# Entry of an MLP: the order of the last norms, where sums of weights are made, and where later columns of weights are put

## The chip, the cores and the metric

The kernel runs on one core of a Trainium2 chip. The metric is the device time of one execution in microseconds, the median of several runs. Before the change it is 1577.01 us (three runs, 1576.17 to 1580.71). The profile is of one further execution of the same program, 1580.5 us, whose span from the first instruction to the last is 1578.7 us.

## The reference

One transformer block in fp32 on 1024 tokens of width 1024: a projection, sparse and sliding-window attention, two gates, an output projection, and an MLP. What matters here is the end:

```python
h = h + rms_norm(y @ w_out[l], norm_mix_post[l])
u = rms_norm(h, norm_mlp_pre[l])
f = jnp.square(jax.nn.relu(u @ w_mlp_in[l])) @ w_mlp_out[l]
h = h + rms_norm(f, norm_mlp_post[l])
```

`w_mlp_in` is 1024 x 4096, `w_mlp_out` 4096 x 1024.

## The kernel before

Every fp32 product is made of three matmuls in the fp32r type: each operand is split into a high part (a copy to fp32r by ScalarE, line L87) and a low part (operand less high part, by VectorE or GpSimd, L91), and high x high, high x low and low x high are added in PSUM. `split` does both. In the names of the rows a final h or l stands for these parts: `ws_h` and `ws_l`, `bh` and `bl`.

The product `u @ w_mlp_in` is done by a scheme with seven products of blocks in place of eight. The right factor is u, transposed, cut into four blocks: upper and lower half of the 1024 rows of the contraction, and first and second 512 tokens. The weights are taken 256 columns at a time; such a *pair* p (16 in all) has two tiles of 128 columns, `raw[0]` and `raw[1]`, each with an upper half (a11, a21) and a lower one (a12, a22). Right factors 1 and 2 are blocks of the first tokens as they are; factors 5, 3, 6, 4 and 7 are made of sums and differences of the blocks. Left factors for 5, 6, 3 and 7 are sums and differences of the weights, four instructions per pair: `ws = a21 + a22` (L1012) and three subtractions (L1039), all on GpSimd. Each product has 12 matmuls of 128 x 128 by 128 x 512. `c11`, `c12`, `c21` and `c22` are the four results of a pair; relu and square follow, and further sums of them (`q`) go to memory as left factors of the second matrix product, which begins when all pairs are done.

In time the part that is changed runs like this. `out_proj` makes the product with `w_out` for blocks of 128 tokens, two at a time. A block b goes through `norm_a` (L854: residual; L856: squares), `norm_b` (L862: the normalised block, tile `o1`, `o` in the rows) and `norm_t` (TensorE's eight transposes L872 into `pt`; for b of 4 to 7 then `t1`, the difference to the block of the first tokens, L881, and copies into `b12` and `b22`, `b_h` and `b_l` in the rows; `t1` is split into factor 5). `factor(i, b)` makes one block of right factor i: 3 is only a split, 6 has two subtractions and a split (L893, L894), 4 one subtraction and a split (L897) and a copy (L899), 7 a split. A product with factor i needs all four blocks of it.

The products 1 and 2 of the first four pairs need the first tokens alone. They are made ahead by `head`, while blocks 4 to 7 are still in the norms: head p splits the first weight tile of pair p, runs the 24 matmuls, adds to get `c11` (L973), takes relu and square in one VectorE instruction (L974), and stores `c11` from SP's queue (L975). Then `mlp1` does the rest of each pair. Pairs 0 and 1 take turns, product by product, with the factors between them; the later pairs follow one by one. `mlp1` loads both tiles of its pair from SP's queue (L1008) into two places each for `wraw` and `wraw2`, so pair 2 loads into what pair 0 used.

The order on each engine is not that of the code. When the program is built, a scheduler places the instructions by their dependencies and by when it thinks that they can run; each engine then works strictly in its own order. SP's queue too: a transfer that waits for its place holds up those behind it. `tc.issue_after(x)` adds one rule: what is written under it stands behind x on x's engine. Tiles of one tag share its `bufs` places in turn: the heads' split weights have two places each for `wh` and `wl`.

Of the kernel before, what the change touches and what calls it, by code (L numbers as in the profile page):

```python
# [52 lines left out]
def tile_hybrid_block(ctx: ExitStack, tc: tile.TileContext, x, norm_mix_pre, norm_mix_post, norm_mlp_pre,  # L53
# [686 lines left out]
    with ExitStack() as s:  # L740
# [99 lines left out]

        ss2s = {}

        def load_x(b, eng=None):
# [15 lines left out]
        def norm_b(b):  # L859

            r2 = rstd_of(ep, ss2s[b])
            nc.vector.scalar_tensor_tensor(o1[b], hbs[b], r2, gpre, op0=ALU.mult, op1=ALU.mult)  # L862

        def norm_t(b):

            t = o1[b]
            bs = slice((b % 4) * P, (b % 4 + 1) * P)
            pts = []
            for k0 in range(0, NB, 4):
                pt = pp.tile([P, 4, P], F32, name="pt", tag="pt", bufs=2)  # L870
                for j in range(4):
                    nc.tensor.transpose(pt[:, j, :], t[:, (k0 + j) * P:(k0 + j + 1) * P], ident)  # L872
                if b < 4:
                    split(bh0[:, k0:k0 + 4, bs], bl0[:, k0:k0 + 4, bs], pt)
                    nc.scalar.activation(braw[b, k0 // 4], pt, AF.Copy)
                pts.append(pt)
            if b < 4:
                return

            t1 = eh.tile([P, 4, P], F32, name="t1", tag="hb", bufs=2)  # L880
            nc.vector.tensor_tensor(t1, pts[0], braw[b % 4, 0], op=ALU.subtract)  # L881
            nc.scalar.activation(b12[:, :, bs], pts[0], AF.Copy)
            nc.scalar.activation(b22[:, :, bs], pts[1], AF.Copy)
            split(bh[5][:, :, bs], bl[5][:, :, bs], t1)
# [59 lines left out]
        norm_a(6)  # L944
        norm_a(7)
        norm_t(4)

# [15 lines left out]
        def head(p, fp_, whl):  # L963
# [9 lines left out]
            nc.vector.tensor_tensor(c11, yb, s1, op=ALU.add)  # L973
            nc.vector.scalar_tensor_tensor(c11, c11, 0.0, c11, op0=ALU.max, op1=ALU.mult)  # L974
            nc.sync.dma_start(f_d[0][p], c11)  # L975
            pre[p] = xb, c11, s1
# [3 lines left out]
        for p in range(NPRE):  # L980
            head(p, fp0, load_wcols(w_mlp_in, 2 * p * P, P, wp2, rpool=wp2, l_eng="dve"))
            if p == 0:
                norm_t(5)
                norm_b(6)
                norm_b(7)
            if p == 1:
                norm_t(6)
                norm_t(7)
        for b in range(4):
            factor(3, b)  # L990
        s_e.close()
# [9 lines left out]

        def mlp1(p):
            raw = []
            for e in range(2):
                r = wp2.tile([P, NB, P], F32, name="wraw", tag="wraw", bufs=2) if e == 0 else \
                    w1a.tile([P, NB, P], F32, name="wraw2", tag="wraw2", bufs=2)
                c0 = (2 * p + e) * P
                nc.sync.dma_start(r, w_mlp_in[:, c0:c0 + P].rearrange("(k p) c -> p k c", p=P))  # L1008
                raw.append(r)
            a11, a12, a21, a22 = raw[0][:, 0:4], raw[0][:, 4:8], raw[1][:, 0:4], raw[1][:, 4:8]  # L1010
            sm = w1a.tile([P, 4, P], F32, name="ws", tag="ws", bufs=3)
            nc.gpsimd.tensor_tensor(sm, a21, a22, op=ALU.add)  # L1012
            early = p in pre
# [24 lines left out]
            for o, i0, i1 in ((sm, sm, a11), (a12, a12, sm), (a21, a11, a21)):  # L1038
                nc.gpsimd.tensor_tensor(o, i0, i1, op=ALU.subtract)  # L1039
            yb = ps_any()  # L1040
# [32 lines left out]
        for i in (6, 4, 7, 0, 0):  # L1073
            for g in two:
                next(g)
            for b in range(4 if i else 0):
                factor(i, b)
        for p in range(2, NPAIR):
# [193 lines left out]
```

## Time and profile before

| | |
|---|---|
| median of 3 runs | 1577.01 us |
| profiled execution | 1580.5 us, span 1578.7 us |
| TensorE busy | 1487.3 us, 94% |
| VectorE busy | 1088.4 us, 69% |
| ScalarE busy | 751.2 us, 48% |
| GpSimd busy | 439.8 us, 28% |
| first head's first matmul | 912.68 us |
| second matrix product of the MLP begins | 1262.36 us |

Busy shares are averages over the whole span. For one stage one asks for the stretch alone: how much of it each engine was busy, which clock TensorE was granted (1.00 is 2.4 GHz, 0.50 is 1.2 GHz), and what ended each idle time. A row in order of time has start, duration, engine, line, operation, out<-in and shapes; in square brackets stands the idle time of the engine before it and what it waited for. The rows of a stretch overlap by some hundredths, since an instruction begins while the one before it still drains; the distance of starts is what an instruction costs.

### The profile page before, as it was taken

What the parts mean: (1) busy time and instruction counts of PE and PEld (TensorE: products, weight loads), DVE (VectorE), ACT (ScalarE), POOL (GpSimd) and SP (SyncE); (2) the same over time, 40 slices, a digit from 0 to 9 for tenths busy, and PEclk for the clock granted to TensorE, in tenths of its full rate; (3) what the DMA queues carried; (4) which work ended last, traced back from release to release, by engine and by line L of the source; (5) the groups of instructions that cost most, each with busy time, mean ns of one, the idle gap of its engine ahead of it and who ended that gap; (6) DMA issues with size and microseconds to landing.
All of it is one profiled execution on the core that took longest, in us unless ns stands there. A gap on an engine that the chain in (4) does not pass through costs nothing. (4 is left out here: it accounts for less than half of the span.)

```text
span 1578.7 us, 20103 instructions
## 1 busy us (share of the span) xinstructions
PE 1487.3 (94%) x6920; PEld 1214.2 (77%) x6920; DVE 1088.4 (69%) x2086; ACT 751.2 (48%) x1461; POOL 439.8 (28%) x354
## 2 busy tenths in 40 slices
PE   6998999999899999999988978999999899999997
PEld 5897888878777777778866766778888688888886
DVE  5455775598964998836537787877757566594775
ACT  5343675576653766653336563332222334334543
POOL 3000351132310232231133014867555410000302
PEclk9999999999999999999999998999999999999999
DMA  7733125111132111164256652444443598263451
GB/s 201 256 103 82 38 51 154 41 44 31 34 97 51 47 34 31 34 225 139 94 186 229 225 159 58 158 162 156 147 153 134 208 336 302 94 188 118 150 184 54
DMA packets 162038, 204.79 MB, mean 130 GB/s; under 512 B 15120, under 2 KB 105264, under 8 KB 161936
## 3 DMA queue, kind: packets, MB, share of 16 engines
q1 hardware_dynamic: 154224, 180.68, 36.5%
q0 software_dynamic: 6992, 20.48, 3.7%
q10 hardware_dynamic: 720, 2.36, 0.4%
q8 instruction: 54, 0.88, 0.2%
q14 instruction: 48, 0.39, 0.1%
HBM read 153.02 MB, written 58.32 MB: 134 GB/s over the span
## 5 line engine op out<-in xcount | busy, mean ns | idle before, releaser
L124 PE MATMUL mm<-uh,wh 128*128 128x512 f32 x464 | 201.4, 434 | 4.1 <-DVE qb L448 3.2
L510 POOL TENSOR_TENSOR e<-e,w 128x256 f32<-128x256 f32 (+7 forms) x128 | 111.6, 898 | 286.4 <-DVE w L648 148.9
L125 PE MATMUL mm<-ul,wh 128*128 128x512 f32 x464 | 184.9, 398 | 0.0
L126 PE MATMUL mm<-uh,wl 128*128 128x512 f32 x464 | 184.5, 398 | 0.0
L87 ACT ACTIVATE th<-pt 128x512 fp32r<-128x512 f32 (+1 forms) x178 | 105.1, 593 | 95.0 <-PE pt L520 84.9
L502 ACT ACTIVATE e<-e,nm 128x256 f32<-128x256 f32 (+7 forms) x192 | 124.4, 649 | 36.8 <-DVE nm L496 36.4
L91 DVE TENSOR_TENSOR tl<-pt,th 128x512 fp32r<-128x512 f32 x162 | 110.0, 682 | 33.8 <-ACT th L87 32.7
L87 ACT ACTIVATE fh<-fraw 128x1024 fp32r<-128x1024 f32 x56 | 59.4, 1062 | 145.3 <-PE xs L1165 78.3
L87 ACT ACTIVATE wh<-wraw 128x1024 fp32r<-128x1024 f32 x69 | 73.0, 1058 | 111.1 <-PE mm L125 36.7
L91 DVE TENSOR_TENSOR fl<-fraw,fh 128x1024 fp32r<-128x1024 f32 x56 | 69.2, 1241 | 78.2 <-ACT fh L87 78.2
L520 PE MATMUL pt<-ident,e 128*128 128x128 f32 x648 | 104.8, 276 | 1.9 <-DVE e L513 0.9
L1165 PE MATMUL xs<-vl,fh 128*128 128x512 f32 x256 | 100.7, 393 | 4.2 <-DVE vl L91 4.2
L126 PEld LDWEIGHTS mm<-uh,wl 128*128 128x128 f32 x464 | 88.0, 190 | 20.9
L124 PEld LDWEIGHTS mm<-uh,wh 128*128 128x128 f32 x464 | 88.9, 192 | 17.4 <-issue 3.3
L91 DVE TENSOR_TENSOR wl<-wraw,wh 128x1024 fp32r<-128x1024 f32 x53 | 69.0, 1301 | 45.9 <-ACT wh L87 45.5
L1165 PE MATMUL xs<-vh,fl 128*128 128x512 f32 x256 | 100.5, 393 | 0.0
L1165 PE MATMUL xs<-vh,fh 128*128 128x512 f32 x256 | 100.2, 392 | 0.0
L1188 POOL TENSOR_TENSOR cc<-cc,gB 128x512 f32<-128x512 f32 x14 | 24.3, 1759 | 269.0 <-ACT sq L1187 267.3
L520 PEld LDWEIGHTS pt<-ident,e 128*128 128x128 f32 x648 | 81.7, 141 | 22.7 <-issue 2.5
L125 PEld LDWEIGHTS mm<-ul,wh 128*128 128x128 f32 x464 | 89.0, 192 | 12.0
L116 POOL TENSOR_TENSOR wl<-wraw,wh 128x384 fp32r<-128x384 f32 (+2 forms) x26 | 38.7, 1493 | 161.7 <-ACT wh L108 161.7
L91 POOL TENSOR_TENSOR wl<-wraw,wh 128x1024 fp32r<-128x1024 f32 x16 | 38.6, 2410 | 159.5 <-ACT wh L87 159.5
(286 smaller groups left out, 4086.0 us busy)
## 6 DMA issues: line engine op xcount, KB each, us to landing
fraw<-f_d SPq DMA_DIRECT2D x48, 512.0 KB, 3.6
wraw<-in_w_mlp_in_dram SPq DMA_DIRECT2D x36, 512.0 KB, 4.5
wraw<-in_w_out_dram SPq DMA_DIRECT2D x32, 512.0 KB, 3.6
f_d<-q SPq DMA_DIRECT2D x64, 256.0 KB, 3.6
b<-in_w_mlp_out_dram SPq DMA_DIRECT2D x32, 512.0 KB, 10.8
wraw<-in_w_in_dram SPq DMA_DIRECT2D x27, 512.0 KB, 4.7
f_d<-c SPq DMA_DIRECT2D x48, 256.0 KB, 4.0
gate_d<-gst SPq DMA_DIRECT2D x32, 256.0 KB, 2.1
```

Source lines behind the costliest of these rows:

```text
L87: nc.scalar.activation(h, src, AF.Copy)
L91: eng.tensor_tensor(l, src, h.bitcast(F32), op=ALU.subtract)
L116: eng.tensor_tensor(lv[:, a:b], rv[:, a:b], hv[:, a:b].bitcast(F32), op=ALU.subtract)
L124: nc.tensor.matmul(ps, ah, bh, start=first, stop=False)
L125: nc.tensor.matmul(ps, ah, bl, start=False, stop=False)
L126: nc.tensor.matmul(ps, al, bh, start=False, stop=last)
L502: nc.scalar.activation(e[:, :n], e[:, :n], AF.Exp, scale=-1.0, bias=nm[:, r:r + 1], accum_out=sm[:, r:r + 1])
L510: nc.gpsimd.tensor_tensor(res[r][:, :n], res[r][:, :n], w[:, r:r + 1].to_broadcast([P, n]), op=ALU.mult)
L520: tr = nc.tensor.transpose(pt[:rows, r, :], es[r][:, off:off + rows], ident)
L1165: nc.tensor.matmul(bank[t], l_[:, j, ts], r_[:, j, :], start=a_, stop=z_, skip_group_check=True)
L1188: (nc.vector if b == NB - 1 else nc.gpsimd).tensor_tensor(cc[:, ns], cc[:, ns], gB[:, ns], op=ALU.mult)
```

## The change

It has four parts.

- `norm_b` of blocks 6 and 7 moves in the code from behind head 0 to the place behind their `norm_a`, and the factors are told to stand behind them on VectorE: factor 3 behind the last `norm_b`, factors 6, 4 and 7 behind the last `t1`.
- For the four early heads, relu and square of `c11` become two instructions on ScalarE, and `c11` is stored from GpSimd's queue.
- The tiles of weights of pairs 0 to 3 are loaded by `load_raw` ahead of all `mlp1`, in the order of the pairs as far as their places allow. Pairs 2 and 3 get places of their own: those of the heads' split weights (`wraw3`, in the tags `wh` and `wl`).
- For pairs 0 and 1 the sum `ws` and the three subtractions run on VectorE, for the others on GpSimd as before.

```diff
@@ -839,6 +839,7 @@
                     nc.vector.tensor_tensor(o1[b][:, ns], pss[t, nh], gpost[:, ns], op=ALU.mult)
 
         ss2s = {}
+        last_norm, last_t = [None], [None]
 
         def load_x(b, eng=None):
             hbs[b] = hb_e[b] if b in hb_e else (eh if b < 4 else ea).tile([P, D], F32, name="hb", tag="hb", bufs=2)
@@ -859,7 +860,7 @@
         def norm_b(b):
 
             r2 = rstd_of(ep, ss2s[b])
-            nc.vector.scalar_tensor_tensor(o1[b], hbs[b], r2, gpre, op0=ALU.mult, op1=ALU.mult)
+            last_norm[0] = nc.vector.scalar_tensor_tensor(o1[b], hbs[b], r2, gpre, op0=ALU.mult, op1=ALU.mult)
 
         def norm_t(b):
 
@@ -878,7 +879,7 @@
                 return
 
             t1 = eh.tile([P, 4, P], F32, name="t1", tag="hb", bufs=2)
-            nc.vector.tensor_tensor(t1, pts[0], braw[b % 4, 0], op=ALU.subtract)
+            last_t[0] = nc.vector.tensor_tensor(t1, pts[0], braw[b % 4, 0], op=ALU.subtract)
             nc.scalar.activation(b12[:, :, bs], pts[0], AF.Copy)
             nc.scalar.activation(b22[:, :, bs], pts[1], AF.Copy)
             split(bh[5][:, :, bs], bl[5][:, :, bs], t1)
@@ -943,6 +944,8 @@
         load_x(7)
         norm_a(6)
         norm_a(7)
+        norm_b(6)
+        norm_b(7)
         norm_t(4)
 
 
@@ -971,8 +974,12 @@
             prod(yb, wh[:, 4:8, :], wl[:, 4:8, :], 2, True, True)
             c11 = fp_.tile([P, 512], F32, name="c11", tag="c11", bufs=NPRE + 1)
             nc.vector.tensor_tensor(c11, yb, s1, op=ALU.add)
-            nc.vector.scalar_tensor_tensor(c11, c11, 0.0, c11, op0=ALU.max, op1=ALU.mult)
-            nc.sync.dma_start(f_d[0][p], c11)
+            if p < NPRE:
+                nc.scalar.activation(c11, c11, AF.Relu)
+                nc.scalar.activation(c11, c11, AF.Square)
+            else:
+                nc.vector.scalar_tensor_tensor(c11, c11, 0.0, c11, op0=ALU.max, op1=ALU.mult)
+            (nc.gpsimd if p < NPRE else nc.sync).dma_start(f_d[0][p], c11)
             pre[p] = xb, c11, s1
 
         s_f0 = s.enter_context(ExitStack())
@@ -981,13 +988,12 @@
             head(p, fp0, load_wcols(w_mlp_in, 2 * p * P, P, wp2, rpool=wp2, l_eng="dve"))
             if p == 0:
                 norm_t(5)
-                norm_b(6)
-                norm_b(7)
             if p == 1:
                 norm_t(6)
                 norm_t(7)
-        for b in range(4):
-            factor(3, b)
+        with tc.issue_after(last_norm[0].ins):
+            for b in range(4):
+                factor(3, b)
         s_e.close()
 
         s_m1 = s.enter_context(ExitStack())
@@ -999,17 +1005,28 @@
             return (p_.tile([P, 4, P], F32R, name=tag + "h", tag=tag + "h", bufs=bufs),
                     p_.tile([P, 4, P], F32R, name=tag + "l", tag=tag + "l", bufs=bufs))
 
-        def mlp1(p):
+        def load_raw(p):
+
             raw = []
             for e in range(2):
-                r = wp2.tile([P, NB, P], F32, name="wraw", tag="wraw", bufs=2) if e == 0 else \
-                    w1a.tile([P, NB, P], F32, name="wraw2", tag="wraw2", bufs=2)
+                if p in (2, 3):
+                    r = wp2.tile([P, NB, P], F32, name="wraw3", tag="wl" if e else "wh", bufs=2)
+                else:
+                    r = (w1a if e else wp2).tile([P, NB, P], F32, name="wraw2" if e else "wraw",
+                                                 tag="wraw2" if e else "wraw", bufs=2)
                 c0 = (2 * p + e) * P
                 nc.sync.dma_start(r, w_mlp_in[:, c0:c0 + P].rearrange("(k p) c -> p k c", p=P))
                 raw.append(r)
+            return raw
+
+        raws = {p: load_raw(p) for p in range(NPRE)}
+
+        def mlp1(p):
+            raw = raws[p] if p in raws else load_raw(p)
             a11, a12, a21, a22 = raw[0][:, 0:4], raw[0][:, 4:8], raw[1][:, 0:4], raw[1][:, 4:8]
             sm = w1a.tile([P, 4, P], F32, name="ws", tag="ws", bufs=3)
-            nc.gpsimd.tensor_tensor(sm, a21, a22, op=ALU.add)
+            diff = nc.vector if p < 2 else nc.gpsimd
+            diff.tensor_tensor(sm, a21, a22, op=ALU.add)
             early = p in pre
             if early:
                 xb, c11, _ = pre[p]
@@ -1036,7 +1053,7 @@
             yield
 
             for o, i0, i1 in ((sm, sm, a11), (a12, a12, sm), (a21, a11, a21)):
-                nc.gpsimd.tensor_tensor(o, i0, i1, op=ALU.subtract)
+                diff.tensor_tensor(o, i0, i1, op=ALU.subtract)
             yb = ps_any()
             prod(yb, *left(3, a12), 3, True, True)
             c12 = ft("c")
@@ -1073,8 +1090,9 @@
         for i in (6, 4, 7, 0, 0):
             for g in two:
                 next(g)
-            for b in range(4 if i else 0):
-                factor(i, b)
+            with tc.issue_after(last_t[0].ins):
+                for b in range(4 if i else 0):
+                    factor(i, b)
         for p in range(2, NPAIR):
             for _ in mlp1(p):
                 pass
```

On VectorE, in the norms of blocks 6 and 7 (`hb_8978` and `o1_8894` belong to block 6, `hb_8980` and `o1_8901` to block 7; `braw` holds the blocks of the first tokens), the kernel before has, from the residual of block 7 on:

```order
L854 SCALAR_TENSOR_TENSOR hb_8980<-o1_8901,rs_o_9008,hb_8980 128x1024
L153 RECIPROCAL rs_o_9095<-rs_a_9093 128x1
L91 TENSOR_TENSOR wl_9220<-wraw_9217,wh_9219 128x1024
L974 SCALAR_TENSOR_TENSOR c11_9143<-c11_9143 128x512
L91 TENSOR_TENSOR bl6_8919<-braw_8028,bh6_8918 128x4x128
L91 TENSOR_TENSOR bl4_8921<-braw_8029,bh4_8920 128x4x128
L894 TENSOR_TENSOR braw_8030<-b_l_8923,braw_8030 128x512
L862 SCALAR_TENSOR_TENSOR o1_8894<-hb_8978,rs_o_9095,gpre_8043 128x1024
L973 TENSOR_TENSOR c11_9213<-ps_9200,s1_9198 128x512
L147 TENSOR_SCALAR rs_t_9100<-ss2_9011 128x1
L149 RECIPROCAL rs_r_9102<-rs_s_9098 128x1
L897 TENSOR_TENSOR braw_8031<-braw_8030,braw_8031 128x512
```

The kernel after has there:

```order
L976 TENSOR_TENSOR c11_9144<-ps_9131,s1_9129 128x512
L863 SCALAR_TENSOR_TENSOR o1_8894<-hb_8978,rs_o_9022,gpre_8043 128x1024
L147 TENSOR_SCALAR rs_t_9027<-ss2_9011 128x1
L91 TENSOR_TENSOR wl_9223<-wraw_9220,wh_9222 128x1024
L149 RECIPROCAL rs_r_9029<-rs_s_9025 128x1
L151 SCALAR_TENSOR_TENSOR rs_a_9031<-rs_r_9029,rs_t_9027,rs_s_9025 128x1
L153 RECIPROCAL rs_o_9033<-rs_a_9031 128x1
L863 SCALAR_TENSOR_TENSOR o1_8901<-hb_8980,rs_o_9033,gpre_8043 128x1024
L91 TENSOR_TENSOR bl3_8917<-b_l_8923,bh3_8916 128x4x128 x2
L976 TENSOR_TENSOR c11_9215<-ps_9202,s1_9200 128x512
```

The last norm of block 7 stood at row 1617 of VectorE and stands at 1597; of the factors, splits and differences of 6 and 4 are behind it now, and factor 3's low parts too.

Behind that, in the kernel after, VectorE has the sums of pairs 0 and 1 (`ws_9295` and `ws_9316`, with `wraw2_9281` and `wraw2_9285` as their second columns) among the last differences `t1` and the splits of factor 5 (`bl5`):

```order
L1029 TENSOR_TENSOR ws_9295<-wraw2_9281 128x512
L1056 TENSOR_TENSOR wraw2_9281<-wraw_9279,wraw2_9281 128x512
L1029 TENSOR_TENSOR ws_9316<-wraw2_9285 128x512
L976 TENSOR_TENSOR c11_9254<-ps_9241,s1_9239 128x512
L91 TENSOR_TENSOR s1_l_9300<-ws_9295,s1_h_9299 128x512
L882 TENSOR_TENSOR t1_9175<-pt_9165,braw_8034 128x512
L894 TENSOR_TENSOR b_l_8923<-b_l_8923,b_h_8922 128x4x128 x3
L1056 TENSOR_TENSOR wraw2_9285<-wraw_9283,wraw2_9285 128x512
L91 TENSOR_TENSOR s1_l_9321<-ws_9316,s1_h_9320 128x512
L1056 TENSOR_TENSOR ws_9295<-ws_9295,wraw_9279 128x512
L91 TENSOR_TENSOR bl3_8917<-b_l_8923,bh3_8916 128x4x128
L895 TENSOR_TENSOR braw_8028<-b_l_8923,braw_8028 128x512
```

The next row is the split of the last block of factor 5. The sums were on GpSimd; the three subtractions on `b_l` are the first of factor 6.

On SP's queue the loads behind the last head's (`wraw_9217`) are these before (`c11_9067` is head 0's):

```order
L975 DMA f0_d_70<-c11_9067 128x512
L1008 DMA wraw_9275<-in_w_mlp_in_dram 128x8x128
L1008 DMA wraw_9300<-in_w_mlp_in_dram 128x8x128
L975 DMA f0_d_70<-c11_9143 128x512
L975 DMA f0_d_70<-c11_9213 128x512
L975 DMA f0_d_70<-c11_9251 128x512
L1008 DMA wraw2_9277<-in_w_mlp_in_dram 128x8x128
L1008 DMA wraw2_9302<-in_w_mlp_in_dram 128x8x128
L1008 DMA wraw_9555<-in_w_mlp_in_dram 128x8x128
L1008 DMA wraw_9674<-in_w_mlp_in_dram 128x8x128
```

and after:

```order
L1018 DMA wraw_9279<-in_w_mlp_in_dram 128x8x128
L1018 DMA wraw_9283<-in_w_mlp_in_dram 128x8x128
L1018 DMA wraw3_9287<-in_w_mlp_in_dram 128x8x128
L1018 DMA wraw2_9281<-in_w_mlp_in_dram 128x8x128
L1018 DMA wraw2_9285<-in_w_mlp_in_dram 128x8x128
L1018 DMA wraw3_9289<-in_w_mlp_in_dram 128x8x128
L1018 DMA wraw3_9291<-in_w_mlp_in_dram 128x8x128
L1018 DMA wraw3_9293<-in_w_mlp_in_dram 128x8x128
L1018 DMA wraw_9797<-in_w_mlp_in_dram 128x8x128
```

The stores of `c11` have gone to another queue; the second columns of pairs 0 and 1 (`wraw2`) stand behind the first load into a head's place (`wraw3_9287`, the first columns of pair 2).

## Rows read from the trace of the kernel before

**Rows 1.** four stretches, busy us (and instructions) by engine; PEclk is the granted clock

```profile
912.00:936.00 24.00, 24.00 (x113) 19.80 (x112) 23.41 (x47) 18.24 (x37) 1.06 (x2) 1.00 0.53 158
936.00:972.00 36.00, 21.88 (x74) 16.02 (x73) 30.51 (x37) 17.18 (x33) 13.30 (x8) 0.72 0.26 73
972.00:1040.00 68.00, 62.51 (x255) 48.15 (x255) 52.55 (x50) 18.55 (x32) 47.55 (x30) 0.97 0.43 137
1040.00:1250.00 210.00, 210.00 (x906) 169.68 (x906) 146.49 (x162) 61.13 (x97) 131.23 (x94) 1.00 0.46 153
```

**Rows 2.** TensorE in order of time: start us, us, line, tiles, idle time before

```profile
930.02 0.39 PE L957 MATMUL ps<-bh,wh 128*128 128x512 f32 x1
...
941.08 1.94 PE L872 MATMUL pt<-ident,o 128*128 128x128 f32 x8 [4.57 <-DVE o L862]
...
947.13 0.80 PE L957 MATMUL ps<-bh,s_h 128*128 128x512 f32 x1 [4.12 <-ACT s_h L87]
...
952.17 0.80 PE L959 MATMUL ps<-bh,s_l 128*128 128x512 f32 x1 [3.81 <-DVE s_l L91]
...
952.76 0.63 PE L957 MATMUL ps<-bh,s_h 128*128 128x512 f32 x1
953.19 0.63 PE L958 MATMUL ps<-bl,s_h 128*128 128x512 f32 x1
```

**Rows 3.** VectorE in order of time, in the entry of the MLP

```profile
919.10 1.28 DVE L854 SCALAR_TENSOR_TENSOR hb<-o,rs_o,hb 128x1024 f32<-128x1024 f32 x1
...
926.74 0.68 DVE L91 TENSOR_TENSOR bl<-t,bh 128x512 fp32r<-128x512 f32 x1
927.34 0.68 DVE L893 TENSOR_TENSOR b_l<-b_l,b_h 128x512 f32<-128x512 f32 x1
...
939.66 1.27 DVE L862 SCALAR_TENSOR_TENSOR o<-hb,rs_o,gpre 128x1024 f32<-128x1024 f32 x1
...
952.64 1.77 DVE L91 TENSOR_TENSOR s_l<-ws,s_h 128x512 fp32r<-128x512 f32 x1
...
954.94 3.47 DVE L91 TENSOR_TENSOR bl<-braw,bh 128x512 fp32r<-128x512 f32 x2
...
962.43 1.28 DVE L91 TENSOR_TENSOR ws_l<-wraw,ws_h 128x512 fp32r<-128x512 f32 x2
```

**Rows 4.** GpSimd in order of time: the first sums of pairs 0 and 2

```profile
944.24 1.70 POOL L1012 TENSOR_TENSOR ws<-wraw 128x512 f32<-128x512 f32 x1 [14.20 <-DMA wraw<-in_w_mlp_in_dram]
...
977.46 1.29 POOL L1012 TENSOR_TENSOR ws<-wraw 128x512 f32<-128x512 f32 x1 [17.90 <-DMA wraw<-in_w_mlp_in_dram]
```

**Rows 5.** SP's queue in order of time: last store of c11, then loads

```profile
939.16 0.32 SPq L975 DMA_DIRECT2D f_d<-c  x1
939.52 36.98 SPq L1008 DMA_DIRECT2D wraw<-in_w_mlp_in_dram  x6
```

**Rows 6.** what TensorE waited for, 972 to 1040: us in total, times, longest

```profile
PE ps L957 <- DVE c L1046: 2.4, 1, 2.4
PE ps L959 <- DVE ws_l L91: 1.4, 2, 1.2
PE ps L957 <- ACT c L1056: 1.2, 1, 1.2
PE ps L957 <- ACT ws_h L87: 0.5, 1, 0.5
```

**Rows 7.** loads issued in 939 to 942, 940 to 941, 975 to 977: us to landing

```profile
wraw<-in_w_mlp_in_dram SPq DMA_DIRECT2D x2, 512.0 KB, 5.2
...
wraw<-in_w_mlp_in_dram SPq DMA_DIRECT2D x1, 512.0 KB, 5.8
...
wraw<-in_w_mlp_in_dram SPq DMA_DIRECT2D x1, 512.0 KB, 4.0
```

**Rows 8.** ScalarE by line, 905 to 1045: count, busy us, mean ns

```profile
L1056 ACT ACTIVATE c<-ps 128x512 f32<-128x512 f32 x4 | 2.4, 594 | 5.1 <-DVE c L1054 5.1
```

## The prediction

> **What bounds the kernel now.** Read the stretches first. From 1040 us on TensorE is busy without a gap, 906 matmuls in 210 us, 0.232 us each [rows 1]. The heads (912 to 936) are full too. What is lost lies between: 255 matmuls in 972 to 1040 would need 59.1 us and take 68, so 8.9 us go there; 936 to 972 has 21.9 busy us of 36 at a mean granted clock of 0.72 [rows 1]. The rest of the kernel only moves along with the entry, since TensorE stays full until 1250, so I look for the gain in these 104 us alone.
>
> TensorE's own rows say what ends the first idle times [rows 2]. The transposes of block 7 wait 4.57 us for o, the normalised block; product 5 waits 4.12 us for s_h, the high part of its weight sum, and 3.81 us more for s_l. From 952.76 to 953.19 matmuls follow at 0.43 us, not 0.232: the granted clock is at its lower level, 1.2 GHz, after these gaps.
>
> Then go to what TensorE waits for. VectorE is busy 30.5 of the 36 us [rows 1], and from its rows [rows 3] the causes are two. First the order: the last norm (L862) starts at 939.66, though its input chain began at 919.10; factors stand between. Second collisions: an instruction on 512 columns follows the one before after 0.60 us (926.74, 927.34), but 1.77 us is spent on one at 952.64 and 3.47 on two at 954.94, while GpSimd works. GpSimd itself could only begin at 944.24, when the second columns of pair 0 had landed [rows 4]: on SP's queue their load stands behind three stores of c11 and goes out at 939.52 [rows 5]. Later, pair 2's sum begins at 977.46, after 17.90 us without its columns [rows 4], and TensorE's waits of 972 to 1040 are 5.5 us in all [rows 6], all on VectorE or ScalarE, which are behind by that.
>
> **The change part by part.** I sum against the profiled execution (1580.5 us, span 1578.7) and carry the difference to the median, 1577.0, which is 3.5 us lower.
>
> *Norms first.* Between the start of L854 for block 6 (919.10) and the last norm, VectorE has, as the order shows, now five instructions of 1024 columns at twice 0.60 us (L854's row has 1.28) and three of 512 at 0.60 ahead of it, 7.8 us and 1 us of small ones; a microsecond for ScalarE's squares makes the last norm start near 929, 11 us earlier than 939.66 [rows 3]. The transposes of block 7 no longer wait: 4.57 us of idle time are freed, but TensorE then waits sooner for the next thing.
>
> *The four c11 edits.* Four VectorE instructions (4 x 0.60 = 2.4 us) become eight on ScalarE, 0.59 us each [rows 8], 4.8 us; ScalarE is busy 17.2 of 36 us there [rows 1], so these hide. Their cover gone, each would push a split by 0.6. The stores go to GpSimd's queue, and nothing reads them before the last stage.
>
> *The loads.* Pair 1's first columns leave when head 3's weights are split, near 928. Behind them now stands pair 2's first half, which waits until TensorE has done with head 2, where head 3 begins, at 930.02 [rows 2]; then the second columns of pairs 0 and 1, near 930.8 and 931.2, not 939.52 and just after. A load alone lands after 4.0 us; of the two issued together at 939.52, the later took 5.8 [rows 7], so about 1.5 us (less than the 1.8 between them) for each one ahead. With two and three ahead I put the landings at 937 and 939. If they ran side by side at the short end, 935; if the queue is slower than these rows, 942.
>
> *The eight sums of pairs 0 and 1 on VectorE.* 8 x 0.60 = 4.8 us come, 2.4 go with c11: VectorE has 49 instructions of 512 columns from 919.10 to the weights of the second pair's product 3, where it had 46 (counted in the order). But until product 5 can run it needs 24, not 36, since the factors 6, 4 and 7 now stand behind the last difference t. It will be stopped at the second landing, 939, with 13 left: 13 x 0.60 = 7.8, and two collisions with GpSimd's first sums of pair 2 at 1.1 (1.77 less 0.68) make 10, so the last low part is there near 949. TensorE begins the run of product 5 at 952.17 now [rows 2]: 3.2 us gained. The bounds are 945 (landing at 935) and 952.
>
> From there 22 more stand before the second pair's low weights: 13.2 us and two collisions, 2.1, so 964.3. In the kernel before, these weights are done at 963.7, as the second of the pair of ws_l that starts at 962.43 [rows 3]. VectorE is thus no earlier at this point; TensorE is, because it has done more of product 3 meanwhile and has ten matmuls (2.3 us) less to make up. I keep 3 us of the first step (from -2, if VectorE's lateness is passed on whole, to 7, the earliest landing).
>
> *The columns of pairs 2 and 3.* They can leave as heads 2 and 3 end, 930 to 937, and land by 943; pair 2's sum can begin some 35 us before 977.46 and the others run while TensorE is at pairs 0 and 1. Then the 8.9 us of 972 to 1040 are free to go. I leave 2.4: one wait of the 1.2 us kind on ws_l [rows 6], as the first split of pair 4 (1.20 us) still stands ahead of pair 3's, and as much for its collisions. So 6.5 us (bounds 0 and 8.9).
>
> Sum: 3 + 6.5 = 9.5 us; 1580.5 - 9.5 = 1571.0 for an execution like the profiled one, 1577.0 - 9.5 = **1567.5 us** for the median.
>
> The collisions first by the rows: a VectorE instruction that reads two operands in SBUF waits for GpSimd's to end, 0.68 becomes 1.77. The Trainium skill (TensorE: Matmul & The Clock Gate, "Why this matters for your kernels") speaks against the change in another place: it advises against idle gaps between bursts of matmuls, which drop the array to half its clock, and the change draws three gaps into one of some 12 us. The trace agrees that gaps cost the clock, 0.43 for 0.232 us after them [rows 2]; what that would come to is the third rival.
>
> **The rivals.**
> 1. *VectorE is the limit at pairs 2 and 3 as well.* For it: 52.6 busy us of 68 in 972 to 1040 [rows 1], with GpSimd at 47.6, and no instruction of pairs 2 and 3 leaves VectorE. Against it: its waits there come in a chain that starts with GpSimd's wait for columns [rows 4]. Then only the small waits go, 1 to 2 us of 8.9: 3 + 1 = 4, 1573.
> 2. *Slower: VectorE carries the sums and the collisions come back.* It is busy 23.4 of the heads' 24 us and 30.5 of the 36 behind them [rows 1]. Place: the stretch up to the second pair's product 3. Price: 3 instructions more (1.8 us), 2.5 us stopped for the second landing, and GpSimd's eight sums for pairs 2 and 3 hitting there as its eight for 0 and 1 did, so that nothing is saved on the 8 x 1.1 us; 4.3 us later. It decides if all eight fall before 968; two of them wait for a split of VectorE itself and four for a buffer of pair 0, which speaks against. With pairs 2 and 3 no better, since VectorE is behind: 1581.
> 3. *The clock stays down.* At 0.43 a matmul costs 0.2 us more. In the kernel before, a mean of 0.72 in 936 to 972 means some 20 us at the lower level [rows 1], 14.1 of them idle, so 6 us, 14 matmuls, paid for it. If short waits keep TensorE at 1.2 GHz through products 5, 3 and 6 of both pairs, 72 matmuls, 58 more pay, 11.6 us; but from 949 to 964.3 TensorE has only 36 matmuls, 8.4 us of work, and 6.9 would have been waiting anyway: 9.5 - 4.7 = 4.8, 1572. For it: in 972 to 1040 no wait is over 2.4 us [rows 6] and the mean clock is 0.97 even so [rows 1]. Against it: a slower TensorE lets VectorE get ahead, so the waits that keep it down vanish.
>
> **How the numbers follow.** Forecast 0.62, with its own range 1563.5 to 1571.5 (landing 935 to 942, and 1.5 to 4 us left at pairs 2 and 3); rival 1 0.22, rival 3 0.09, rival 2 0.07. The range reaches from 1562.5, the early landing together with nearly all of the 8.9, to 1574.5, which takes in rivals 1 and 3. A measurement of this kernel can tell 0.3%, 4.7 us, from no change: faster means below 1572.3. The forecast lies there wholly, rivals 1 and 3 with a little under half: 0.76. Rival 2 and the tail of rival 1 give slower 0.06, the rest, 0.18, is the same.
>
> **What would show it.** Right: the last norm near 929; no wait of the block 7 transposes; one gap of TensorE, from about 937 to 949, ended by a bl or s_l of VectorE; the sums of pair 0 on VectorE preceded by idle time that a DMA ends, near 937; GpSimd's first sum near 941, for pair 2; and in the 68 us that follow matmul 60 after the heads, TensorE idle under 3 us. Wrong: product 5 starting after 952 (the landing was mis-sized), a second low clock of more than 4 us (rival 3), or waits on ws_l of pairs 2 and 3 summing to over 5 us (rival 1). If the transposes of block 7 still wait for o, the reordering did not do what it says.

## The result and the profile after

The changed kernel takes 1568.59 us (median, 1567.05 to 1569.34), the kernel before, run beside it, 1576.85 us: ratio 0.9941, 95% interval 0.9924 to 0.9959, a gain of 8.3 us by the medians. The profiled execution took 1569.34 us, its span is 1567.6.

The two profiled executions differ by more than the entry. The heads' first matmul starts at 912.68 us before and at 909.32 after, though the change lies behind it; over the twelve traces of this document it lies between 906.90 and 914.01. The profile of before was that of the longest of its runs. From here on times are counted from that matmul ("at +39"), and the matmuls of the products are numbered from it: 96 begins product 5, pairs 0 and 1 are through at 216, pairs 2 and 3 at 336. From 400 on both kernels need the same (220.0 us to matmul 1343). I call the stretch up to matmul 240 the first step, and give 240 to 400 to pairs 2 and 3.

The stretches after, which answer to [rows 1]:

```profile
912.00:936.00 24.00, 22.42 (x111) 18.57 (x110) 18.35 (x38) 17.06 (x36) 2.69 (x5) 1.00 0.80 235
936.00:972.00 36.00, 20.90 (x69) 16.14 (x70) 35.63 (x48) 20.41 (x37) 11.74 (x9) 0.72 0.26 76
972.00:1040.00 68.00, 68.00 (x293) 54.78 (x293) 55.16 (x63) 22.98 (x36) 46.78 (x31) 1.00 0.42 140
1040.00:1241.00 201.00, 201.00 (x867) 162.39 (x866) 129.54 (x151) 56.36 (x89) 119.99 (x87) 1.00 0.45 152
```

In 972 to 1040 TensorE is full now (68 of 68, clock 1.00): the whole of the 8.9 us is back. In 936 to 972 it is not better, 20.90 busy us for 21.88, and VectorE has no gap left there (35.63 of 36). Since the heads start 3.4 us earlier in this trace, the same place counted from them, +26 to +60, is the fairer stretch; first before, then after:

```profile
938.68:972.68 34.00, 22.06 (x72) 16.30 (x73) 28.49 (x33) 15.46 (x28) 13.30 (x8) 0.70 0.26 70
...
935.32:969.32 34.00, 18.22 (x58) 13.97 (x59) 33.18 (x46) 19.77 (x36) 9.86 (x7) 0.70 0.30 86
```

TensorE does less there, at the same mean clock. All of TensorE's waits from 905 to 1060, in us, times, longest (for [rows 6]):

```profile
PE ps L960 <- ACT p L1034: 13.8, 1, 13.8
PE ps L962 <- DVE ws_l L91: 2.3, 1, 2.3
PE ps L960 <- ACT wh L87: 0.7, 1, 0.7
PE ps L960 <- DVE p L1052: 0.6, 1, 0.6
```

In order of time, for [rows 2]:

```profile
948.26 0.80 PE L960 MATMUL ps<-bh,s_h 128*128 128x512 f32 x1 [13.84 <-ACT p L1034]
...
962.42 0.80 PE L962 MATMUL ps<-bh,ws_l 128*128 128x512 f32 x1 [2.26 <-DVE ws_l L91]
963.01 0.63 PE L960 MATMUL ps<-bh,ws_h 128*128 128x512 f32 x1
963.44 0.63 PE L961 MATMUL ps<-bl,ws_h 128*128 128x512 f32 x1
...
968.56 0.40 PE L961 MATMUL ps<-bl,ws_h 128*128 128x512 f32 x1
968.80 0.40 PE L962 MATMUL ps<-bh,ws_l 128*128 128x512 f32 x1
```

The three waits of before (4.57, 4.12, 3.81) are one of 13.84. It ends with ScalarE's copy of product 5's PSUM bank (p, L1034), so follow ScalarE's rows:

```profile
947.01 0.63 ACT L87 ACTIVATE bh<-braw 128x512 fp32r<-128x512 f32 x1 [5.32 <-DVE braw L895]
947.61 1.09 ACT L1034 ACTIVATE p<-ps 128x512 f32<-128x512 f32 x2
```

The copies stand behind a factor's high part, which waited for VectorE (L895). VectorE in order of time, for [rows 3]:

```profile
925.47 1.28 DVE L863 SCALAR_TENSOR_TENSOR o<-hb,rs_o,gpre 128x1024 f32<-128x1024 f32 x1
...
935.78 0.69 DVE L1029 TENSOR_TENSOR ws<-wraw 128x512 f32<-128x512 f32 x1 [3.39 <-DMA wraw<-in_w_mlp_in_dram]
...
937.53 0.69 DVE L1029 TENSOR_TENSOR ws<-wraw 128x512 f32<-128x512 f32 x1 [0.33 <-DMA wraw<-in_w_mlp_in_dram]
...
939.94 4.03 DVE L894 TENSOR_TENSOR b_l<-b_l,b_h 128x512 f32<-128x512 f32 x3
...
946.90 0.68 DVE L91 TENSOR_TENSOR bl<-t,bh 128x512 fp32r<-128x512 f32 x1
...
960.62 1.75 DVE L91 TENSOR_TENSOR ws_l<-wraw,ws_h 128x512 fp32r<-128x512 f32 x1
```

The last norm starts at +16.2 (before +27.0), but VectorE then stands still for the second columns of pairs 0 and 1, which land at +26.5 and +28.2. Behind that three subtractions of factor 6 (L894; the expectations below call them additions) take 4.03 us, where three undisturbed ones took 1.89 in later runs. Just there GpSimd starts on pair 2 (for [rows 4]):

```profile
939.88 1.26 POOL L1029 TENSOR_TENSOR ws<-wraw 128x512 f32<-128x512 f32 x1 [6.86 <-DMA wraw<-in_w_mlp_in_dram]
941.22 1.59 POOL L1056 TENSOR_TENSOR wraw<-wraw,wraw 128x512 f32<-128x512 f32 x1
...
958.50 1.64 POOL L1056 TENSOR_TENSOR ws<-ws,wraw 128x512 f32<-128x512 f32 x1 [15.19 <-DVE s_l L91]
960.23 1.59 POOL L1056 TENSOR_TENSOR wraw<-wraw,ws 128x512 f32<-128x512 f32 x1
```

The last two meet VectorE again: its row at 960.62 is the low part of the weights of the second pair's product 3, 1.75 us long, and TensorE's wait of 2.26 us ends 0.05 us after it.

Product 5 starts at +38.9 instead of +34.5. It then runs in one piece, matmul 98 (the first with a low weight) stands at +40.0 for +39.5, and matmul 240 at +80.3 for +78.7. From 240 to 400 the kernel needs 37.2 us for 46.1. So the first step **lost** 1.5 us and pairs 2 and 3 gained 8.8. Between matmul 132 (at +48.9 for +52.9, 4.0 us ahead) and 240 the lead was lost: that stretch needs 31.35 us for 25.88. Of the 5.5 us more, 3.3 go with two waits (0.58 and 2.26 idle). Nearly all of the rest is the clock: until 968.56, 14 matmuls go at the 0.43 us of the lower level (1.2 GHz), which is 2.9 us more than at 0.233 each; before, it was three, 0.6 us more.

### The profile page after: what moved, and what is told of

It reads as the page before. It is cut to its first block, busy times and chain, and to the rows that moved or that the text cites. A ratio compares the mean times of both kernels' runs of the same rounds, so it can differ in the third digit from the quotient of the medians.

```text
span 1567.6 us, 20118 instructions
## 1 busy us (share of the span) xinstructions
PE 1479.0 (94%) x6920; PEld 1209.2 (77%) x6920; DVE 1075.5 (69%) x2090; ACT 756.1 (48%) x1469; POOL 425.1 (27%) x350
## 4 chain that ended last, share of the span: by engine, by line
PE 45%; DMA 5%; DVE 4%; ACT 2%; issue 1%; POOL 1%; DVEq 0%; SPq 0%; ACTq 0%; POOLq 0%
PE xs L1183 10%; PE ys L1183 8%; PE ps L962 6%; PE ps L960 6%; PE ps L961 6%; DMA wraw<-in_w_out_dram 4%; PE ps L126 2%; PE ps L125 2%; PE ps L124 2%; DMA wraw<-in_w_mlp_in_dram 1%; POOL wl L116 1%; DVE wl L91 1%; PE mm L124 1%; PE mm L125 1%; PE mm L126 1%
## 5 line engine op out<-in xcount | busy, mean ns | idle before, releaser
L91 DVE TENSOR_TENSOR fl<-fraw,fh 128x1024 fp32r<-128x1024 f32 x56 | 69.4, 1242 | 77.3 <-ACT fh L87 77.1
L1206 POOL TENSOR_TENSOR cc<-cc,gB 128x512 f32<-128x512 f32 x14 | 24.3, 1764 | 268.3 <-ACT sq L1205 266.6
L87 ACT ACTIVATE ws_h<-wraw 128x512 fp32r<-128x512 f32 x48 | 30.3, 632 | 120.4 <-PE ps L961 120.1
```

The lines of the kernel that those rows point to most:

```text
L87: nc.scalar.activation(h, src, AF.Copy)
L91: eng.tensor_tensor(l, src, h.bitcast(F32), op=ALU.subtract)
```

## The experiments

Theory at the start: the gain is the early columns of pairs 2 and 3; the first step lost because the queue of transfers that these columns join made the second columns late. Rivals: the gain is the sums on VectorE; or what costs the first step is GpSimd's early work on pair 2.

The results, five rounds for each experiment. The ratio is to the kernel before on the same chip, whose median was 1575.45 to 1577.41 us in these series; the last three columns are from each one's trace: the places of matmuls 96 and 240, in us from the heads' first matmul, and the time from 240 to 400.

| kernel | median us | ratio (95%) | 96 | 240 | 240 to 400 |
|---|---|---|---|---|---|
| before | 1576.85 | | 34.5 | 78.7 | 46.1 |
| after | 1568.59 | 0.9941 (0.9924, 0.9959) | 38.9 | 80.3 | 37.2 |
| no_columns | 1569.36 | 0.9946 (0.9929, 0.9963) | 34.6 | 72.0 | 44.7 |
| columns_only | 1572.71 | 0.9974 (0.9962, 0.9985) | 36.3 | 84.9 | 37.2 |
| sums_pool | 1569.00 | 0.9949 (0.9935, 0.9964) | 39.3 | 79.7 | 38.1 |
| no_order | 1564.87 | 0.9923 (0.9906, 0.9939) | 34.2 | 75.5 | 37.2 |
| sums_only | 1569.83 | 0.9967 (0.9955, 0.9979) | 35.2 | 71.4 | 44.9 |
| second_early | 1565.15 | 0.9933 (0.9920, 0.9945) | 35.2 | 72.3 | 39.3 |
| dve4 | 1564.25 | 0.9928 (0.9916, 0.9939) | 37.0 | 74.3 | 38.0 |
| dve4_early | 1560.16 | 0.9906 (0.9893, 0.9918) | 33.4 | 69.1 | 38.1 |
| no_after_t | 1565.44 | 0.9924 (0.9910, 0.9937) | 38.3 | 74.1 | 37.5 |
| best_no_order | 1562.72 | 0.9908 (0.9893, 0.9922) | 31.0 | 73.9 | 37.2 |

Of the kernels that differ from the changed one by a single part, none has an interval that lies wholly below the changed kernel's; what 3 to 5 us are due to is read from the traces, one for each kernel. The times set apart from it only dve4_early and best_no_order, which are faster, and columns_only, which is slower. They bear the traces out to some 3 us: the median less the place of matmul 400 is 1450.6 to 1453.9 us for all twelve.

**no_columns**: columns of pairs 2 and 3 late again.

```diff
-                if p in (2, 3):
-                    r = wp2.tile([P, NB, P], F32, name="wraw3", tag="wl" if e else "wh", bufs=2)
-                else:
+                if True:
...
-        raws = {p: load_raw(p) for p in range(NPRE)}
+        raws = {p: load_raw(p) for p in range(2)}
```

> The changed kernel, but the columns of pairs 2 and 3 are loaded late, into the old places, as before the change. Theory (the gain is early columns of pairs 2 and 3; the queue of transfers that they make costs 1.5 us at pair 0): TensorE's idle time between the first step of pairs 2, 3 and the later pairs comes back (8.9 us by the two traces), and the second columns of pairs 0 and 1 land about 2 us earlier than 35.78 us on the trace's clock, so that product 5 starts 2 to 3 us earlier after the heads' first matmul than the 38.9 us of the changed kernel. Time 1568.6 + 8.9 - 1.5 to 3 = 1574.5 to 1576. Rival (the gain is the sums on VectorE, which leave GpSimd free for pairs 2 and 3): GpSimd is still free, the time stays at 1568.6 to 1570.

The time is the one that the rival gave, but not for its reason. Pairs 2 and 3 lose 7.5 us (37.2 to 44.7), as the theory said, though GpSimd is free until +58. The first step gains 8.3, which I had put at 1.5 to 3, and the two cancel. Its VectorE rows (heads from 908.76), with the landing at +23.0 and no GpSimd work beside the subtractions, are these:

```profile
931.78 0.69 DVE L1027 TENSOR_TENSOR ws<-wraw 128x512 f32<-128x512 f32 x1 [2.75 <-DMA wraw<-in_w_mlp_in_dram]
...
937.20 1.89 DVE L894 TENSOR_TENSOR b_l<-b_l,b_h 128x512 f32<-128x512 f32 x3
```

Its GpSimd waits for pair 2's columns as it did before the change:

```profile
966.96 1.29 POOL L1027 TENSOR_TENSOR ws<-wraw 128x512 f32<-128x512 f32 x1 [28.34 <-DMA wraw<-in_w_mlp_in_dram]
```

And TensorE then waits for the weights of pairs 2 and 3 (975 to 1035, us in total, times, longest):

```profile
PE ps L962 <- DVE ws_l L91: 3.1, 2, 2.8
PE ps L960 <- ACT ws_h L87: 0.8, 1, 0.8
```

**columns_only**: the kernel before with the early columns of pairs 2 and 3 (load_raw and its calls) and nothing else.

> The kernel before with the early columns of pairs 2 and 3 alone: sums of pairs 0, 1 stay on GpSimd, the last norms, the factors and the heads' relu-square stay where they were. Theory (early columns alone make the gain of 8.9 us, less what the queue costs the first step): the time is near the changed kernel's, 1568 to 1571. Rival (early columns are worth nothing while GpSimd still carries the sums of pairs 0 and 1: its sums of pair 2 stand behind them): 1575 to 1577, and TensorE's waits for the low weights of pairs 2 and 3 stay.

Between the two. Pairs 2 and 3 gain all of it without any other part (46.1 to 37.2), so the sums on VectorE are not what frees them; but the first step loses 6.1 us, from +78.7 to +84.9. GpSimd's first sum starts 2.4 us later (+33.9 for +31.6). GpSimd then works without a pause from 940.85 to 957.6, and VectorE's rows beside it read like this one after another:

```profile
943.02 1.66 DVE L893 TENSOR_TENSOR b_l<-b_l,b_h 128x512 f32<-128x512 f32 x1
944.60 1.75 DVE L91 TENSOR_TENSOR s_l<-ws,s_h 128x512 fp32r<-128x512 f32 x1
946.27 1.77 DVE L894 TENSOR_TENSOR braw<-b_l,braw 128x512 f32<-128x512 f32 x1
```

**sums_pool**: sums of pairs 0 and 1 on GpSimd again.

```diff
-            diff = nc.vector if p < 2 else nc.gpsimd
+            diff = nc.gpsimd
```

> The changed kernel with one line undone: the weight sums of pairs 0 and 1 are on GpSimd again. Theory: the sums on VectorE stand behind the landing of the second columns and then hold up VectorE's low split of factor 5, but GpSimd must wait for the same landing and takes 2 to 3 times as long a sum, and its subtractions wait behind it; the first step of pairs 0, 1 ends 2 to 5 us later and the second step's waits stay away: 1570.5 to 1573.5. Rival 1 (VectorE is the worse place, since it holds up the factor): 1566 to 1567.5. Rival 2 (GpSimd's load brings the waits for pairs 2 and 3 back): 1575 to 1577.

None of the three: 1569.00 us, no different from the changed kernel (ratios 0.9949 and 0.9941, intervals nearly the same), with 240 at +79.7. With the other parts in place, this part is worth nothing that can be measured.

**sums_only**: the kernel before with that one part alone (the sums and subtractions of pairs 0 and 1 on VectorE).

> The kernel before with the sums and subtractions of pairs 0 and 1 on VectorE, and nothing else: loads, last norms and factors as before. Theory: the three parts of the change stand in for one another at the first step: sums on VectorE end the long instructions there (GpSimd is idle until pair 2), matmul 240 stands 4 to 6 us earlier than 78.7 us, but the late columns of pairs 2 and 3 then cost 7 to 8 us as in no_columns: 1571 to 1574. Rival (moved work without the last norms ahead of it is worth nothing, since VectorE is the bound until the last norm): 1576 to 1578.

The same part alone is worth 7.3 us at the first step in the trace and 5.2 us in the time (0.9967; interval 3.3 to 7.1), a little more than expected (1569.83 us, below the 1571 to 1574 of the theory); the late columns then take 7.7 at pairs 2 and 3 (44.9 for 37.2). Its last norm starts at +27.8, that of no_columns, which has the two orders, the c11 edits and an earlier landing (+23.0; the first sum of sums_only stands at +32.4) as well, at +16.6: 11.2 us earlier, and product 5 starts 0.5 us earlier (34.6 for 35.2), 240 0.5 later (72.0 for 71.4). **An earlier last norm, with all that came with it, gained nothing at the first step.** No run has the norms' place alone against sums_only.

**no_order**: both orders of the change undone (norms back behind norm_t(5), factors free).

```diff
-        norm_b(6)
-        norm_b(7)
...
                 norm_t(5)
+                norm_b(6)
+                norm_b(7)
...
-        with tc.issue_after(last_norm[0].ins):
-            for b in range(4):
-                factor(3, b)
+        for b in range(4):
+            factor(3, b)
...
-            with tc.issue_after(last_t[0].ins):
-                for b in range(4 if i else 0):
-                    factor(i, b)
+            for b in range(4 if i else 0):
+                factor(i, b)
```

> The changed kernel with the two orders undone: the last norms stand behind the transposes of block 5 again, and the right factors may stand ahead of them. Columns and sums as in the changed kernel. Theory (the last norm at 25.5 instead of 39.7 us on the trace's clock does what it was worth, but its gain went to the landing of the second columns): the last transposes start later by what the norm is later, the sums by as much, and the time is 2 to 3 us longer, 1570.5 to 1572. Rival (the order is what cost the first step: it sends VectorE's copy of the factors and the norms ahead of the weights that the heads need): 3 to 5 us shorter, 1564 to 1566.

The theory fell, the rival held: 1564.87 us (the intervals of the two kernels overlap), and matmul 400 at +112.7 where the changed kernel has +117.5. The second columns land later still (sum at 942.07, +32.3, after a wait of 1.12), but VectorE has factors to do until then.

**no_after_t**: the norms stay ahead; only the second order, the last hunk above, is undone.

> The changed kernel with one of its two orders undone: the last norms stay ahead of factor 3, but factors 6, 4 and 7 need no longer stand behind the last subtraction of block 7. With both undone (no_order) the time was 3.7 us shorter and matmul 240 stood at 75.5 us after the heads' first matmul, not 80.3. If VectorE's time while it waits for the second columns is what the order wastes (3.39 us in the changed kernel's row of the first sum), the factors fill that wait: matmul 240 at 75 to 77 us, 1564 to 1566. If the norms ahead of factor 3 are the part that costs: 1568 to 1569.

As expected, 1565.4 us, with 240 a little earlier than that, at +74.1. The first sum's wait shrinks from 3.39 to 0.99 us (heads from 911.40), five instructions of factors 6 and 4 standing ahead of it now. The order of factors 6, 4 and 7 behind the last t is thus what costs, by the traces; the norms ahead cost nothing (no_order, without them, has 240 at +75.5). Product 5 starts only 0.6 us earlier than in the changed kernel (+38.3), but the second pair's low weights of product 3 are there at +46.7 instead of +53.1, TensorE waits for none of them, and matmuls 132 to 240 need 25.2 us instead of 31.35. The rows of its first sum and of these low weights:

```profile
936.58 0.69 DVE L1029 TENSOR_TENSOR ws<-wraw 128x512 f32<-128x512 f32 x1 [0.99 <-DMA wraw<-in_w_mlp_in_dram]
...
957.39 0.68 DVE L91 TENSOR_TENSOR ws_l<-wraw,ws_h 128x512 fp32r<-128x512 f32 x1
```

The next three separate the two costs of the early columns at the first step: late landing and shared time.

**second_early**: SyncE's loads in another order (without the hunk that lets load_raw load one half and note its last transfer).

```diff
-        raws = {p: load_raw(p) for p in range(NPRE)}
+        raws = {p: {} for p in range(NPRE)}
+        for p in (0, 1):
+            raws[p].update(load_raw(p, (1,)))
+        with tc.issue_after(last_load[0].ins):
+            for p in (0, 1):
+                raws[p].update(load_raw(p, (0,)))
+        with tc.issue_after(last_load[0].ins):
+            for p in (2, 3):
+                raws[p].update(load_raw(p))
```

> The changed kernel with SyncE's loads in another order: the second columns of pairs 0 and 1 first, then their first columns, then the columns of pairs 2 and 3. With late columns of pairs 2 and 3 (no_columns) the sum's columns landed 23.0 us after the heads' first matmul and product 5 started at 34.6 us; in the changed kernel 26.5 and 38.9 us. Theory 1 (the queue of transfers makes the landing late): the columns land 2.5 to 3.5 us earlier, product 5 starts as much earlier, time 1565 to 1566.5. Theory 2 (what costs is the shared time of GpSimd's sum of pair 2 with VectorE, 2.1 us on the three factor additions): the landing is earlier but product 5 starts within 1 us of 38.9, time 1567.5 to 1569.

Theory 1: 1565.15 us, product 5 at +35.2. The sum stands at +20.5 with no wait, and the subtractions still meet GpSimd (heads from 914.01):

```profile
934.52 0.68 DVE L1038 TENSOR_TENSOR ws<-wraw 128x512 f32<-128x512 f32 x1
...
940.89 2.95 DVE L894 TENSOR_TENSOR b_l<-b_l,b_h 128x512 f32<-128x512 f32 x3
943.76 1.74 DVE L1065 TENSOR_TENSOR wraw<-wraw,wraw 128x512 f32<-128x512 f32 x1
```

**dve4**: sums and subtractions of pairs 2 and 3 on VectorE too (`p < 4` for `p < 2` in the line of sums_pool); loads as in the changed kernel.

> The changed kernel with the sums and subtractions of pairs 2 and 3 on VectorE too, so that GpSimd has no tensor work in the first step; loads as in the changed kernel. Theory 1 (landing): product 5 still starts 38 to 39 us after the heads' first matmul; time 1567.5 to 1569. Theory 2 (shared time): the three factor additions take 1.9 us instead of 4.03, product 5 starts 2 us earlier, the wait of 2.3 us for the second pair's low weights goes, time 1564.5 to 1566.5. Rival from the prediction (VectorE becomes the bound at pairs 2 and 3, with 8 instructions of 0.6 us more): waits of TensorE for VectorE after 75 us, time 1570 or more.

Theory 2 as well: 1564.25 us, product 5 at +37.0, and the subtractions at 1.88 us although the sum waits 3.09 us for its columns. Pairs 2 and 3 need 38.0 us for 37.2: the rival from the prediction, VectorE as the bound there, is refuted even with eight more instructions on it.

```profile
935.23 0.69 DVE L1029 TENSOR_TENSOR ws<-wraw 128x512 f32<-128x512 f32 x1 [3.09 <-DMA wraw<-in_w_mlp_in_dram]
...
939.32 1.88 DVE L894 TENSOR_TENSOR b_l<-b_l,b_h 128x512 f32<-128x512 f32 x3
```

**dve4_early**: both.

> Both together: loads in the order of second_early, all eight sums and subtractions of pairs 2 and 3 on VectorE. If landing and shared time are the two parts of the 8.3 us that the early columns cost the first step (matmul 240 at 80.3 us after the heads' first instead of 72.0), both come back and matmul 400 stands at 109 to 111 us instead of 117.5: time 1560.5 to 1562.5, below both kernels. If VectorE becomes the bound with the added 5 us of work: 1566 or more.

1560.16 us, below both kernels; its interval lies wholly below the changed kernel's. The two costs add up. At product 5 the earlier landing is worth 3.75 us (38.94 to 35.19) or 3.64 (37.00 to 33.36), the unshared time 1.94 or 1.83, and both together 5.58. At matmul 400 it is 5.9 and 5.1, and 10.3 together (117.5 to 107.2), earlier than the 109 to 111 I expected. TensorE has one wait of weight left, 8.72 us (13.84 in the changed kernel, and 2.26 behind it):

```profile
946.52 0.80 PE L960 MATMUL ps<-bh,s_h 128*128 128x512 f32 x1 [8.72 <-ACT p L1043]
```

Its stretch from +26 to +60 answers to 18.22 busy us at a clock of 0.70 in the changed kernel:

```profile
939.16:973.16 34.00, 26.64 (x105) 21.32 (x106) 34.00 (x58) 20.07 (x37) 0.66 (x2) 0.85 0.32 89
```

**best_no_order**: dve4_early without the two orders.

> dve4_early (loads of the second columns first, all sums of pairs 0 to 3 on VectorE, 1560.2 us) with the last norms and factors in the order of the kernel before. From sums_only to no_columns the last norm came 11.2 us earlier and product 5 only 0.5 us, so the order would be worth nothing: 1559.5 to 1561.5, matmul 240 within 1.5 us of 69.4. If the order pays once the second columns are there in time (the last norm releases the places that they load into): matmul 240 at 72 to 76, 1562.5 to 1566.

By the trace the second branch: product 5 2.4 us earlier (+31.0), but 240 4.8 us later (+73.9 for +69.1; the 69.4 of the expectation is the place of matmul 241), since TensorE then stops 3.41 us for the first pair's low weights of product 3. That matmul 240 is later is shown by these two traces; the reason that the expectation gives, places that the norm releases, is not. The times can't tell it: 0.9908 against 0.9906.

## Why the prediction was right, and where it was not

1567.5 us forecast, 1568.59 measured; faster, as forecast. The sum came out by two errors of opposite sign: 3 + 6.5 = 9.5 forecast; by the traces -1.5 + 8.8 = 7.3, by the times 8.3. That it hit the total so closely is luck.

- *The columns of pairs 2 and 3*: mechanism right, the term too small: 8.8 instead of 6.5. No wait of TensorE was left from 240 to 400, so the 2.4 that I held back was not needed. columns_only shows that this part alone gives it.
- *Norms first*: the last norm at +16.2, where I had 929 on the clock of before (+16.3), and the wait of block 7's transposes gone. But its worth was nothing that shows: where it came 11.2 us earlier, and the second columns too (no_columns against sums_only), product 5 gained 0.5.
- *The four c11 edits*: no run undoes them alone, so whether they hid is not shown.
- *The loads*: this step failed by size. I put the landings at 937 and 939 on the clock of before, +24.3 and +26.3; they were at +26.5 and +28.2. They left when I had said, at +18.1 and +18.7, but took 8.3 and 9.5 us where I had counted 6.2 and 7.8, at 1.5 us for each load ahead. second_early shows that the loads ahead were worth 3.7 us at product 5.
- *The sums on VectorE*: 24 instructions until product 5, two collisions and a stop for the landing were all there. Behind these 24 the trace has 22 to the second pair's low weights, as counted, so 46 in all; that is as many as before, not the 49 that the prediction set against 46. The last low part (946.90) was there at +38.3, 1.9 later than the 949 (+36.3) of the prediction, as the late landing makes it. After it one thing I had not counted: product 5 also needs ScalarE's copy of its bank, which stood behind a factor's high part, and so started at +38.9.
- *The 3 us that I kept for the first step*: the step that failed. My own count had VectorE reach the second pair's low weights at 964.3 (+51.6), later than the 963.7 (+51.0) of before, and I credited TensorE with ten matmuls less to make up. The low weights were done at 962.37 (+53.1), 1.4 later than my count, since the landing was late, and TensorE, 4.0 us ahead at matmul 132, waited 2.26 us there and then paid the lower clock: a lead over an engine that one waits for is worth nothing. The loss of 1.5 us lies near my lower bound of -2, VectorE's lateness passed on whole.
- *Rival 2, collisions come back*: right in kind. They come back twice, 4.03 us where 1.89 would do, at the place it named, and cost 1.9 us at product 5; and twice more just before the second pair's low weights, where the two instructions of 959.53 and 960.62 cost 1.56 us more than 0.60 each. They do not come with all eight sums, so the sign held.
- *Rival 3, the clock*: its sign, a second low clock of more than 4 us, did come, from 962.42 to 968.56 behind the wait of 2.26 (a mean of 0.66 in 960 to 970). Over the first step as a whole it took little more than before: from matmul 96 to 240 it cost 4.4 us over 0.233 a matmul, 3.8 before. But 2.9 of them lie behind the last wait, from matmul 132 on (0.6 before), where they are passed on whole. The Trainium skill (TensorE: Matmul & The Clock Gate, "Why this matters for your kernels") advises against idle gaps between bursts of matmuls. The traces agree: behind the gap of 13.84 us 7 matmuls followed at the lower level, behind that of 2.26 us 14; dve4_early, with one gap of 8.72 us, has 10 behind it and none later in the first step, 0.85 in the stretch for 0.70.

The change as a whole: its parts stand in each other's way. Sums on VectorE alone give 7.3 us at the first step, and early columns alone 8.8 at pairs 2 and 3, less 6.1 at the first step; together with the orders, 7.3 in all, because the columns take 8.3 back at the first step (no_columns against after: +72.0 and +80.3). What the first step lost was shown by the traces to be landing, shared time and an order that lets VectorE stand idle; for landing and shared time together the times show it too (dve4_early). The 2.26 us and the lower clock behind it do not follow from product 5's lateness alone: no_after_t starts it only 0.6 us earlier and has neither. Not settled: what the orders alone would do in the kernel before, which was not run; and whether they pay in the best version, 4.0 us at matmul 400 by one trace each, unresolved by the times.

## What to carry to other kernels

A prefetch is paid for by the loads that it overtakes: put what is needed first at the head of the queue, and look at which engine its earlier landing wakes up and whose time that engine shares. An order that puts one engine's work behind a load leaves that engine idle if the load is late; leave it something to fill in. And when a producer sets the pace, finishing the consumer's earlier work sooner is no gain: compare the producer's own time at the next handover, not the consumer's.

## What the runs showed of the hardware

Loads of 512 KB that stand in line take longer to land. In the changed kernel the only load of weights issued between 924.5 and 926.5 landed after 4.5 us, but the three issued from 927 to 929 after 8.3 (median):

```profile
wraw<-in_w_mlp_in_dram SPq DMA_DIRECT2D x1, 512.0 KB, 4.5
...
wraw<-in_w_mlp_in_dram SPq DMA_DIRECT2D x3, 512.0 KB, 8.3
```

The DMA engines then moved 291 GB/s, and the view puts their busy share at 1.03:

```profile
928.00:941.00 13.00, 6.42 (x37) 5.32 (x35) 7.49 (x11) 7.38 (x14) 1.66 (x2) 0.88 1.03 291
```

With the order of second_early the three issued from 928 to 934 took 6.3. So the 4.0 to 5.8 us of [rows 7] held for loads with little beside them. As an estimate from these rows, 512 KB at 291 GB/s are 1.8 us for each load ahead: 4.0 us and two or three of these make 7.6 and 9.4, near the 8.3 and 9.5 measured.

A VectorE instruction on two operands in SBUF took 1.66 to 1.77 us instead of 0.68 while GpSimd ran one on SBUF. The Trainium skill (GPSIMD Engine Reference, "1. Specifications") says that the two engines contend for an interface when VectorE has two SBUF inputs; the subtractions of factor 6 agree, 4.03, 2.95 and 1.89 us for three with two, one and no meeting, 1.07 us each.
